# A two-layer trunk of matrix products: first stages in another order, and every large tile at a multiple of 512 bytes

## The chip, the cores and the metric

The kernel runs on one core of a Trainium2 chip. The metric is the device time of one execution in microseconds, lower is better. Before the change it is 2411.27 us, the median of three runs from 2409.95 to 2413.39.

## What is computed

Two layers work on 512 tokens of width 1024, all in float32. Each layer normalises x, projects it once into everything that follows, runs two token mixers on that (retention with four heads, and sparse attention with sixteen heads of width 64 in two groups), merges both by gates, adds the result to x and ends with a gated feed-forward part of width 2816. Cut to what matters:

```
h = rms_norm(x, norm_mix_g[i]);  proj = h @ w_in[i]
q_r, k_r, v_r, g_r, q_n, kv_n, gate_n, m_a, m_b = split(proj)
y_ret = (silu(g_r) * group_norm(retention(rotary(q_r), rotary(k_r), v_r))) @ w_o_ret[i]
y_nsa = nsa(q_n, kv_n (6 parts: compressed, selected, window keys and values), sigmoid(gate_n), ...) @ w_o_nsa[i]
x = x + (sigmoid(m_a) * y_ret + sigmoid(m_b) * y_nsa) @ w_out[i]
a, b = split(rms_norm(x, norm_ffn_g[i]) @ w_ffn_in[i])
x = x + (silu(a) * b) @ w_ffn_out[i]          # after two layers: rms_norm(x, norm_final_g)

def compress(kv, pos_emb, w1, w2):            # 31 overlapping blocks of 32 tokens
    flat = (blocks(kv) + pos_emb).reshape(..., 31, 32 * 64)
    return gelu(flat @ w1) @ w2
```

## The kernel before

Activations lie transposed: a tile holds 128 of the 1024 features (one of eight, called k) in its partitions and the 512 tokens along the free axis. Every product of float32 data is three matmuls (`mm3`, L122 to L124): each operand is split into a rounded part and the rest (hi and lo), and hi·hi, hi·lo and lo·hi are added up in one bank of PSUM. A product of 1024 features with 128 columns of weights is so 24 matmuls of 128x512. The split is `split` (L79 a copy on ScalarE, L80 a subtraction on VectorE), or `split_scaled` (L83, L84), which multiplies by the gain of the norm as well. The norm's other factor, one number per token, is applied behind the products by a multiplication with `rb`, a tile that holds it for all partitions. `norm_stats` makes the factor out of the summed squares (matmuls against ones, L216, and a power on GpSimd, L220), `norm_bcast` spreads it (a copy to `rep` on VectorE, L225, and four transposes on TensorE, L229).

Weights are loaded through SyncE's DMA queue (SP) into three buffers `wr` of up to 1 MB (`raw`, L91) and split into `wh` and `wl`, three buffers each (`cut`). Working tiles of 2 KB per partition share 37 slots (tag "u"); other tags (`p`, `pt`, `strip`, `mt`, `ld`, `cv`, `ks`) have their own. Within a partition the slots of "u", `p`, `pt` and `ks` begin 416 bytes past a multiple of 512, the weight buffers 96 past one, and `strip`, `mt`, `ld` and `cv` 160 past one: small tiles that are placed ahead of them set this.

The order of the work on each engine is settled when the program is built, by a scheduler that gives each engine its instructions in a row by their dependences and its own estimates; `issue_after` adds a dependence of order. The program's own order is the following. `start_x` (L232) loads x and the first weights (the 256 columns whose keys and values are compressed) and splits them. `nsa_kv` (L261) then makes the two products `psc` (banks "f"), calls `self.stats[0]` (bias rows at L176, squares by `acc_sq`, `norm_stats`), makes the key products `psk` (banks "a") with `norm_bcast` between them, and takes turns between the two compressions (`compress`, L323, for "k" and "v", whose matmuls are L362) and 18 steps of the first quad's q projection (`nsa_q`, L410, through `fill`). Each compression first builds z (L337) and xa (L348) on VectorE and splits xa into the tiles that its matmuls read. After that the sixteen heads run, four of them (a quad) on one q projection each; `nsa_q` gives for each half of a quad a hi and a lo tile of which one half of the partitions comes from a split, and the other half is copied from the first by L431. The first to read them are L441 and L442 in `nsa_cmp`. The bias of each head is a strip of 256 KB loaded on SP (L188). Retention, mixing and the feed-forward part follow; `proj_n` (L717) has the weights moving and the activations as stationary tile, all others the reverse.

Of the kernel before, what the change touches and what calls it, by code (L numbers as in the profile page):

```python
# [8 lines left out]
F32 = mybir.dt.float32  # L9
F32R = mybir.dt.float32r  # L10
AF = mybir.ActivationFunctionType
ALU = mybir.AluOpType
AX = mybir.AxisListType

P = 128
T = 512
D = 1024
NT = T // P
KD = D // P
# [3 lines left out]
HN = 16  # L23
# [8 lines left out]
class Builder:  # L32
# [86 lines left out]
    def mm3(self, ps, items, start=True, stop=True):  # L119
        n = len(items)  # L120
        for i, (lh, ll, rh, rl) in enumerate(items):
            self.nc.tensor.matmul(ps, lh, rh, start=start and i == 0, stop=False)  # L122
            self.nc.tensor.matmul(ps, lh, rl, start=False, stop=False)  # L123
            self.nc.tensor.matmul(ps, ll, rh, start=False, stop=stop and i == n - 1)  # L124

    def proj_t(self, w, j, acts, bank=None):

# [5 lines left out]
    def setup(self):  # L133
        nc, a = self.nc, self.a
        self.bv = self.dr.tile([HN, 640], F32, tag="bv", name="bv")
        self.cols = self.const("cols", [P, 104])
        nc.sync.dma_start(self.cols, a["c_cols"])
        self.gmix = [self.cols[:, l * 8 : l * 8 + 8] for l in range(DEPTH)]
        self.gffn = [self.cols[:, 16 + l * 8 : 24 + l * 8] for l in range(DEPTH)]
        self.pos = {"k": [self.cols[:, 40 + l * 16 : 56 + l * 16] for l in range(DEPTH)],  # L140
                    "v": [self.cols[:, 72 + l * 16 : 88 + l * 16] for l in range(DEPTH)]}
        self.ident = self.const("ident", [P, P])
        nc.gpsimd.dma_start(self.ident, a["c_ident"])
        self.setup_bias()
        self.mhalf = self.const("mhalf", [P, NT])
        nc.vector.memset(self.mhalf, -0.5)
        self.ones = self.const("ones", [P, 1])
        nc.vector.memset(self.ones, 1.0)
        self.rb = self.const("rb", [P, T])
        self.rstd = self.const("rstd", [P, NT])  # L150
        self.hrstd = self.const("hrstd", [P, NT])
        self.kcz = [self.const(f"kcz{g}", [P, 224], F32R) for g in range(2)]
        for g in range(2):
            nc.vector.memset(self.kcz[g].bitcast(F32), 0.0)
        self.xs = self.dr.tile([KD, P, T], F32, tag="xs", name="xs")
        self.gs = self.dr.tile([2 * KD, P, T], F32, tag="gs", name="gs")
        self.gr = self.dr.tile([4 * NSPILL, P, T], F32, tag="gr", name="gr")
        self.ys = self.dr.tile([KD, P, T], F32, tag="ys", name="ys")
        self.cmask = self.const("cmask", [P, NT, 32])
        nc.gpsimd.dma_start(self.cmask, a["c_cmask"].rearrange("p (i n) -> p i n", n=32))  # L160
# [71 lines left out]
    def start_x(self):  # L232

        nc = self.nc
        xts = [self.u("xt") for _ in range(KD)]
        w = self.a["w_in"][0][:, C_KV : C_KV + 256].rearrange("(k p) n -> p k n", p=P)
        for k in range(2):
            last = nc.sync.dma_start(xts[k], self.a["c_xt"][k])
        with self.tc.issue_after(last.ins):
            raw = self.raw([(lambda v: v, w)], KD, 256)  # L240
        with self.tc.issue_after(self.last_load.ins):
            for k in range(2, KD):
                self.last_x = nc.sync.dma_start(xts[k], self.a["c_xt"][k])
        h = [self.make_h(xts[k], self.gmix[0][:, k : k + 1]) for k in range(2)]
        with self.tc.issue_after(self.last_hi.ins):
            self.first_w = [self.cut(raw[:, :, j * P : (j + 1) * P]) for j in range(2)]
        h += [self.make_h(xts[k], self.gmix[0][:, k : k + 1]) for k in range(2, KD)]
        self.first_h = self.last_hi

        def stats():  # L250
            self.bias_rows()
            acc = None
            for xt in xts:
                acc = self.acc_sq(acc, xt)
            self.norm_stats(acc)

        self.stats = stats, self.norm_bcast
        return h


    def nsa_kv(self, l, h, q0):  # L261
        nc, w = self.nc, self.a["w_in"][l]
        view = lambda c, n, k0=0, kt=KD: w[k0 * P : (k0 + kt) * P, c : c + n].rearrange("(k p) n -> p k n", p=P)
        wc = self.first_w if l == 0 else self.wcols(w, 0, KD, C_KV, 256)
        psc = [self.proj_t(wc, j, h, "f") for j in range(2)]
        with self.tc.issue_after(self.last_x.ins) if l == 0 else nullcontext():
            wk = self.raw([(lambda v: v[:, :, :P], view(C_KV + 256, P)), (lambda v: v[:, :, P:], view(C_KV + 512, P))], KD, 256)
        self.stats[0]()
        nc.vector.tensor_scalar(self.hrstd, self.rstd, 0.5, None, ALU.mult)
        ks = [self.sb.tile([P, 2, T], F32R, tag=f"ks{g}", name=self.nm("ks"), bufs=1) for g in range(2)]  # L270

        def keys(br):
            kd, kh = self.u("kd"), self.u("kh", F32R)
            nc.vector.tensor_tensor(kd, psk[br], self.rb, ALU.mult)
            lo, hi = slice(0, 64), slice(64, P)
            self.split(ks[0][lo, br], ks[0][hi, br], kd[lo])
            self.split(kh[hi], ks[1][hi, br], kd[hi])
            nc.scalar.activation(ks[1][lo, br], kd[hi], AF.Copy)

        def values(half):  # L280
            return self.chunk([(lambda v: v[:, :, 0:P], view(C_KV + 384, P, half * 4, 4)),
                               (lambda v: v[:, :, P : 256 + 48], view(C_KV + 640, P + 48, half * 4, 4))], 4, 304, "k")

        with self.tc.issue_after(self.first_h.ins) if l == 0 else nullcontext():
            wk = [self.cut(wk[:, :, br * P : (br + 1) * P]) for br in range(2)]
        psk = [self.proj_t(wk, 0, h, "a")]
        self.stats[1]()
        psk.append(self.proj_t(wk, 1, h, "a"))
        comp = {kind: self.compress(l, kind, psc[i]) for i, kind in enumerate("kv")}
        fill = lambda n: [next(q0, None) for _ in range(n)]  # L290
        next(comp["k"])
        fill(9)
        next(comp["k"])
        next(comp["k"])
        next(comp["v"])
        keys(0)
        fill(9)
        next(comp["v"])
        next(comp["v"])
        keys(1)  # L300
        vs = [self.sb.tile([P, 4, 2, 64], F32R, tag="u", name=self.nm("vs")) for _ in range(NT)]
        gate = self.sb.tile([P, NT, HN, 3], F32, tag="gate", name=self.nm("gate"), bufs=1)
        pss = [self.bank(b) for b in "aaoo"]
        for half in range(2):
            wv = values(half)
            for t in range(NT):
                ts = slice(t * P, (t + 1) * P)
                self.mm3(pss[t][:, :304], [(h[half * 4 + k][0][:, ts], h[half * 4 + k][1][:, ts], wv[k][0], wv[k][1])
                                           for k in range(4)], start=half == 0, stop=half == 1)
            if half == 0:  # L310
                for kind in "kv":
                    next(comp[kind], None)
        for t in range(NT):
            src = pss[t][:, :256].rearrange("p (b d) -> p b d", d=64)
            rc = self.rstd[:, t : t + 1]
            nc.scalar.activation(vs[t][:, :, 0, :], src, AF.Copy, scale=rc)
            nc.vector.scalar_tensor_tensor(vs[t][:, :, 1, :], src, rc, vs[t][:, :, 0, :].bitcast(F32), ALU.mult, ALU.subtract)
            gt = gate[:, t].rearrange("p h b -> p (h b)")
            nc.scalar.activation(gt, pss[t][:, 256:304], AF.Tanh, scale=self.hrstd[:, t : t + 1])
            nc.vector.tensor_scalar(gt, gt, 0.5, 0.5, ALU.mult, ALU.add)  # L320
        return ks, vs, gate
# [88 lines left out]
    def nsa_q(self, l, h, quad, qs):  # L410
# [7 lines left out]
        for a in range(2):  # L418
# [7 lines left out]
            for g in range(2):  # L426
# [1 line left out]
                r, o = (slice(x * 64, x * 64 + 64) for x in (g, 1 - g))  # L428
                self.split(hi[r], lo[r], d[r])
                for x in (hi, lo):  # L430
                    nc.scalar.activation(x[o], x[r].bitcast(F32), AF.Copy)  # L431
                qs.append((hi, lo))
            yield

# [468 lines left out]
    def last_ffn(self, l, x, h):  # L903
# [3 lines left out]
        for hf in range(2):  # L907
            gf.append(self.tile("p", NPB))
            nc.sync.dma_start(gf[hf], self.a["norm_final_g"][None, hf * 512 : hf * 512 + 512].broadcast_to([P, 512]))
        ss = self.small("ss", 2 * NT)  # L910
        base = self.small("base", NT)
        for k0, kt in GROUPS:
            hid = self.hidden(l, h, k0, kt)
# [59 lines left out]
WR = 3  # L973
WH = 3
# [4 lines left out]
AT = {"scores": (0, 0.5), "values": (0, 0.8), "finish": (0.6, 0.6), "fill": (0.1, 0.7)}  # L979
QAT = (2, 2)  # L980
NSPILL = 3
FILL = [20, 18, 8, 8, 14, 14, 8, 8, 14, 14, 8, 8, 14, 14, 14, 14, 14, 12]
BANKS = {"a": 2, "o": 2, "t": 2, "f": 2}
CYCLE = "afo"
# [65 lines left out]
```

## Time and profile before

| | |
|---|---|
| median of three runs | 2411.27 us |
| the profiled execution | 2411.87 us |
| its span (first to last instruction) | 2409.8 us |
| TensorE busy | 2364.8 us, 98% |
| weight loads of TensorE | 1936.3 us, 80% |
| VectorE busy | 1386.1 us, 58% |
| ScalarE busy | 1070.7 us, 44% |
| GpSimd busy | 258.2 us, 11% |
| mean rate of the DMA engines | 108 GB/s |

Matmuls are pipelined, and their ends are modelled: one of 128x512 is shown with some 0.39 us, while the next starts earlier than that. The time that a stream of them needs is read from the distance between two starts, and not from the durations.

### The profile page before, as it was taken

The numbers are of one execution on the slowest core, as the hardware profiler recorded it, in microseconds if no ns is written. First come the engines' busy times: TensorE is split into PE (matmuls) and PEld (weight loads), VectorE is DVE, ScalarE is ACT, GpSimd is POOL, SyncE is SP. The second block draws the span as 40 slices with busy tenths as digits, with TensorE's granted clock in tenths as the row PEclk, the third lists the DMA queues.
The fourth block names the chain that finished last, engine by engine and source line by source line (L and its number), as shares of the span: only waits on it lengthen the run. The fifth ranks groups of instructions, "written<-read, shape, count | busy, mean of one in ns | idle before, by whom it ended". The sixth has DMA issues, their size and how long they took to land.

```text
span 2409.8 us, 29134 instructions
## 1 busy us (share of the span) xinstructions
PE 2364.8 (98%) x11042; PEld 1936.3 (80%) x11042; DVE 1386.1 (58%) x2715; ACT 1070.7 (44%) x1926; POOL 258.2 (11%) x224
## 2 busy tenths in 40 slices
PE   7999999999999999999989999999999999999998
PEld 5887778888887888888878777788888878888887
DVE  6777887354574633333577877864555754434344
ACT  5677786233333422222356777742433343322222
POOL 3000000010030110110200000001100202101010
PEclk9999999999999999999999999999999999999999
DMA  7532223522342522323444232244232533223221
GB/s 210 143 89 74 74 83 93 183 75 95 106 159 86 163 88 91 101 90 98 142 142 129 81 84 70 78 130 147 92 92 92 179 107 130 89 87 105 88 96 61
DMA packets 234172, 260.35 MB, mean 108 GB/s; under 512 B 42214, under 2 KB 178438, under 8 KB 234033
## 3 DMA queue, kind: packets, MB, share of 16 engines
q1 hardware_dynamic: 220688, 236.93, 32.3%
q10 hardware_dynamic: 13152, 21.37, 2.4%
q8 instruction: 86, 1.41, 0.2%
q14 instruction: 54, 0.43, 0.1%
q0 software_dynamic: 192, 0.21, 0.0%
HBM read 235.36 MB, written 23.11 MB: 107 GB/s over the span
## 4 chain that ended last, share of the span: by engine, by line
PE 90%; ACT 4%; DVE 4%; issue 1%; POOL 1%; DMA 0%; SPq 0%; ACTq 0%; POOLq 0%
PE f L122 12%; PE f L123 12%; PE f L124 12%; PE a L123 8%; PE a L122 8%; PE o L122 8%; PE o L123 8%; PE o L124 8%; PE a L124 8%; PE t L564 2%; PE o L556 1%; PE o L557 1%; ACT wh L79 1%; PE a L529 1%; PE a L530 1%
## 5 line engine op out<-in xcount | busy, mean ns | idle before, releaser
L79 ACT ACTIVATE wh<-wr 128x1024 fp32r<-128x1024 f32 (+3 forms) x406 | 397.9, 980 | 952.9 <-PE f L123 227.5
L80 DVE TENSOR_TENSOR wl<-wr,wh 128x1024 fp32r<-128x1024 f32 (+3 forms) x406 | 465.7, 1151 | 227.2 <-ACT wh L79 224.9
L122 PE MATMUL f<-hh,wh 128*128 128x512 f32 x936 | 373.1, 399 | 3.2 <-ACT wh L79 3.2
L123 PE MATMUL f<-hl,wh 128*128 128x512 f32 x936 | 369.9, 395 | 0.0
L124 PE MATMUL f<-hh,wl 128*128 128x512 f32 x936 | 368.1, 394 | 1.2 <-DVE wl L80 1.1
L124 PEld LDWEIGHTS f<-hh,wl 128*128 128x128 f32 x936 | 176.4, 188 | 41.9 <-DVE wl L80 3.6
L122 PEld LDWEIGHTS f<-hh,wh 128*128 128x128 f32 x936 | 176.4, 188 | 37.7 <-ACT wh L79 5.0
L123 PEld LDWEIGHTS f<-hl,wh 128*128 128x128 f32 x936 | 176.6, 189 | 30.7
L511 ACT ACTIVATE p<-p,nmx 128x512 f32<-128x512 f32 (+3 forms) x256 | 142.5, 557 | 53.7 <-DVE nmx L510 51.2
L80 DVE TENSOR_TENSOR pt<-t,pt 128x512 fp32r<-128x512 f32 (+3 forms) x256 | 123.2, 484 | 50.6 <-ACT pt L79 49.3
L874 POOL TENSOR_TENSOR fa<-fa,rb 128x512 f32<-128x512 f32 x44 | 77.6, 1763 | 562.2 <-ACT fa L873 562.2
L510 DVE CUSTOM_DVE_ANT_0 p<-a,strip 128x512 f32<-128x512 f32 (+3 forms) x256 | 119.4, 483 | 25.2 <-PE a L530 15.6
L123 PE MATMUL a<-hl,wh 128*128 128x512 f32 x336 | 132.4, 394 | 0.0
L122 PE MATMUL a<-hh,wh 128*128 128x512 f32 x336 | 132.4, 394 | 0.0
L124 PE MATMUL a<-hh,wl 128*128 128x512 f32 x336 | 131.2, 390 | 0.0
L79 ACT ACTIVATE pt<-t 128x512 fp32r<-128x512 f32 (+3 forms) x256 | 109.1, 427 | 47.6 <-PE t L564 43.5
L123 PE MATMUL o<-hl,wh 128*128 128x512 f32 x328 | 129.2, 394 | 0.0
L122 PE MATMUL o<-hh,wh 128*128 128x512 f32 x328 | 129.0, 393 | 0.0
L124 PE MATMUL o<-hh,wl 128*128 128x512 f32 x328 | 127.9, 390 | 0.0
L564 PE MATMUL t<-ident,p 128*128 128x128 f32 x640 | 113.9, 273 | 0.0
L564 PEld LDWEIGHTS t<-ident,p 128*128 128x128 f32 x640 | 81.2, 140 | 23.6 <-DVE pt L80 1.7
L556 PE MATMUL o<-pt,vs 128*128 128x512 f32 (+3 forms) x256 | 92.8, 365 | 3.2 <-ACT pt L79 3.2
(405 smaller groups left out, 4842.7 us busy)
## 6 DMA issues: line engine op xcount, KB each, us to landing
wr<-in_w_in SPq DMA_DIRECT2D x66, 1024.0 KB, 5.3
wr<-in_w_ffn_in SPq DMA_DIRECT2D x44, 1024.0 KB, 5.1
wr<-in_w_ffn_out SPq DMA_DIRECT2D x18, 1024.0 KB, 5.0
wr<-in_w_o_ret SPq DMA_DIRECT2D x16, 1024.0 KB, 5.0
wr<-in_w_in SPq DMA_DIRECT2D x36, 256.0 KB, 4.6
strip<-bv SPq DMA_DIRECT2D x32, 256.0 KB, 4.0
gs<-mt ACTq DMA_DIRECT2D x32, 256.0 KB, 2.0
wr<-in_w_o_nsa SPq DMA_DIRECT2D x16, 512.0 KB, 6.5
```

The lines of the kernel that those rows point to most:

```text
L79: self.nc.scalar.activation(hi, src, AF.Copy)
L80: (eng or self.nc.vector).tensor_sub(lo, src, hi.bitcast(F32))
L122: self.nc.tensor.matmul(ps, lh, rh, start=start and i == 0, stop=False)
L123: self.nc.tensor.matmul(ps, lh, rl, start=False, stop=False)
L124: self.nc.tensor.matmul(ps, ll, rh, start=False, stop=stop and i == n - 1)
L510: nc.vector.tensor_tensor_reduce(p, src, self.backwards(strip, w - 1, w), -1.0, BIG, ALU.add, ALU.min, nmx[:, c])
L511: nc.scalar.activation(p, p, AF.Exp, scale=-1.0, bias=nmx[:, c], accum_out=sm[:, c])
L529: nc.tensor.matmul(ps[:, :w], qh[:, ts], ks[:, br, :w], start=True, stop=False)
L530: nc.tensor.matmul(ps[:, :w], ql[:, ts], ks[:, br, :w], start=False, stop=True)
L556: nc.tensor.matmul(po[:, j * P :], lhs, th, start=br == 0 and j == 0, stop=False)
L564: nc.tensor.transpose(pt[:, (i - j) * P : (i - j + 1) * P], pr[br][i][:, j * P : (j + 1) * P], self.ident)
L874: nc.gpsimd.tensor_mul(t, t, self.rb)
```

## The change

The program is changed in six places.

1. Three pads (a constant of 96 bytes, a small tile of 48 floats, and `gate` widened to 256 floats), with one buffer number fixed (`ss`), move all large tiles to a multiple of 512 bytes within a partition.
2. At the start stand 32 matmuls of 224 columns on the zeroed tile `kcz`, whose result nobody reads; and a small copy on ScalarE (`hrstd`) comes before its other work.
3. `start_x` loads the first weights in four pieces of 256 KB between the x tiles, splits them in pairs of k, and `nsa_kv` goes through k with both banks instead of through one bank after the other (in layer 0).
4. In layer 0 the squares are added on VectorE instead of GpSimd; the norm's matmuls and the bias rows follow the first key product, the transposes the first half of the second. In layer 1 both stand between the two products `psc`.
5. In the compression stage v's blocks are built before k's third step, and the keys are written out later.
6. The 64 copies of q halves become DMAs on SP (L464 after the change).

```diff
 def setup(self):
+        self.const("pad", [P, 24])
+        self.small("pad", PAD, bufs=1)
         self.hrstd = self.const("hrstd", [P, NT])
+        nc.scalar.activation(self.hrstd, self.mhalf, AF.Copy)
+        ps = self.tp()
+        for _ in range(IDLE):
+            nc.tensor.matmul(ps[:, :224], self.kcz[0][:, :P], self.kcz[1], start=True, stop=True)
...
 def start_x(self):
-        for k in range(2):
-            last = nc.sync.dma_start(xts[k], self.a["c_xt"][k])
-        with self.tc.issue_after(last.ins):
-            raw = self.raw([(lambda v: v, w)], KD, 256)
+        for k in range(KD):
+            with order():
+                if k % 2 == 0:
+                    nc.sync.dma_start(raw[:, k : k + 2], w[:, k : k + 2])
+                xts.append(self.u("xt"))
                 self.last_x = nc.sync.dma_start(xts[k], self.a["c_xt"][k])
+            order = lambda: self.tc.issue_after(self.last_x.ins)
...
         def stats():
-            self.bias_rows()
             for xt in xts:
-                acc = self.acc_sq(acc, xt)
+                sq = self.u("sq")
+                nc.scalar.activation(sq, xt, AF.Square)
+                if acc is not None:
+                    nc.vector.tensor_add(sq, acc, sq)
+                acc = sq
             self.norm_stats(acc)
+            self.bias_rows()
...
 def nsa_kv(self, l, h, q0):
-        psc = [self.proj_t(wc, j, h, "f") for j in range(2)]
+        if l == 0:
+            psc = [self.bank("f") for _ in range(2)]
+            for k in range(KD):
+                for j in range(2):
+                    wh, wl = (v[:, j * P : (j + 1) * P] for v in self.first_w[k])
+                    self.mm3(psc[j], [(wh, wl, *h[k])], start=k == 0, stop=k == KD - 1)
+        else:
+            wc = self.wcols(w, 0, KD, C_KV, 256)
+            psc = [self.proj_t(wc, 0, h, "f")]
+            self.stats[0]()
+            psc.append(self.proj_t(wc, 1, h, "f"))
+            self.stats[1]()
-        self.stats[0]()
         psk = [self.proj_t(wk, 0, h, "a")]
-        self.stats[1]()
-        psk.append(self.proj_t(wk, 1, h, "a"))
+        if l == 0:
+            with self.tc.issue_after(self.last_mm.ins):
+                self.stats[0]()
+        psk.append(self.bank("a"))
+        for half in range(2):
+            part = range(4 * half, 4 * half + 4)
+            self.mm3(psk[1], [(wk[1][0][:, k], wk[1][1][:, k], *h[k]) for k in part], start=half == 0, stop=half == 1)
+            if l == 0 and half == 0:
+                with self.tc.issue_after(self.last_mm.ins):
+                    self.stats[1]()
         next(comp["k"])
         fill(9)
         next(comp["k"])
+        next(comp["v"])
         next(comp["k"])
-        next(comp["v"])
-        keys(0)
         fill(9)
         next(comp["v"])
         next(comp["v"])
+        keys(0)
         keys(1)
-        gate = self.sb.tile([P, NT, HN, 3], F32, tag="gate", name=self.nm("gate"), bufs=1)
+        gate = self.tile("gate", 1, w=256)[:, : NT * HN * 3].rearrange("p (t h b) -> p t h b", t=NT, h=HN)
...
 def nsa_q(self, l, h, quad, qs):
                 for x in (hi, lo):
-                    nc.scalar.activation(x[o], x[r].bitcast(F32), AF.Copy)
+                    nc.sync.dma_start(x[o].bitcast(F32), x[r].bitcast(F32))
...
+PAD = 48
+IDLE = 32
```

Three places show how instructions move. The first is SP's queue at its beginning (`cols` holds the gains; the numbers behind names count tiles), before:

```order
L137 DMA cols<-c_cols 128x104
L238 DMA xt_99<-c_xt 128x512
L238 DMA xt_100<-c_xt 128x512
L91 DMA wr_109<-in_w_in 128x8x256
L243 DMA xt_101<-c_xt 128x512
```

and after the change:

```order
L138 DMA cols<-c_cols 128x104
L248 DMA wr_135<-in_w_in 128x2x256
L250 DMA xt_137<-c_xt 128x512
L250 DMA xt_139<-c_xt 128x512
L248 DMA wr_135<-in_w_in 128x2x256
L250 DMA xt_142<-c_xt 128x512
```

The one load of 1 MB has become four of 256 KB, each ahead of two x tiles.

The second is VectorE in layer 0's compression stage, where the blocks of "v" are built (z and xa) and q's weights are split (wl); before, the last weight splits stand among z's operations and ahead of xa:

```order
L80 TENSOR_TENSOR ql_397<-qd_388,qh_396 64x512
L80 TENSOR_TENSOR wl_508<-wr_354,wh_507 128x1024
L369 TENSOR_TENSOR gx_455<-o_402,gy_456 64x256
L80 TENSOR_TENSOR wl_554<-wr_551,wh_553 128x1024
L371 TENSOR_SCALAR gy_456<-gy_456 64x256
L337 TENSOR_TENSOR z_466<-f_182,rb 64x256
L372 TENSOR_TENSOR gy_456<-gy_456,gx_455 64x256
L337 TENSOR_TENSOR z_466<-f_182,rb 64x256 x2
L374 SCALAR_TENSOR_TENSOR gy_456<-gy_456,gx_455 64x256
L337 TENSOR_TENSOR z_466<-f_182,rb 64x256
L348 TENSOR_TENSOR xa_471<-z_466,cols 128x4x31 x2
```

and after the change:

```order
L80 TENSOR_TENSOR ql_440<-qd_431,qh_439 64x512
L370 TENSOR_TENSOR z_474<-f_201,rb 64x256 x4
L381 TENSOR_TENSOR xa_479<-z_474,cols 128x4x31 x2
L381 TENSOR_TENSOR xa_486<-z_474,cols 128x4x31 x2
L381 TENSOR_TENSOR xa_493<-z_474,cols 128x4x31
L80 TENSOR_TENSOR pt_483<-xa_479,pt_483 128x4x64
L80 TENSOR_TENSOR pt_490<-xa_486,pt_490 128x4x64
L381 TENSOR_TENSOR xa_493<-z_474,cols 128x4x31
L381 TENSOR_TENSOR xa_500<-z_474,cols 128x4x31 x2
L402 TENSOR_TENSOR gx_533<-o_445,gy_534 64x256
L80 TENSOR_TENSOR pt_497<-xa_493,pt_497 128x4x64
L80 TENSOR_TENSOR pt_504<-xa_500,pt_504 128x4x64
```

wl_543, the split of the weights for q's second half, follows two rows further down (before, wl_508 has that place).

The third is SP's queue in the same stage, where the q copies (qh, ql) come in; before:

```order
L188 DMA strip_1424<-bv 128x512
L91 DMA wr_551<-in_cmp_w_v 128x8x256
L91 DMA wr_577<-in_cmp_w_v 128x8x256
L91 DMA wr_629<-in_w_in 128x4x128
L91 DMA wr_629<-in_w_in 128x4x176
```

and after the change:

```order
L91 DMA wr_586<-in_cmp_w_v 128x8x256
L195 DMA strip_1465<-bv 128x512
L195 DMA strip_1467<-bv 128x512
L464 DMA qh_433<-qh_433 64x512
L464 DMA ql_434<-ql_434 64x512
L464 DMA qh_439<-qh_439 64x512
L91 DMA wr_612<-in_cmp_w_v 128x8x256
L464 DMA ql_440<-ql_440 64x512
L91 DMA wr_672<-in_w_in 128x4x128
```

Four copies of the first quad's first half now stand ahead of or between the next weight loads.

## Rows read from the trace of the kernel before

**Rows 1.** The page: span, and each engine's busy time, share and instructions

```profile
span 2409.8 us, 29134 instructions
PE 2364.8 (98%) x11042; PEld 1936.3 (80%) x11042; DVE 1386.1 (58%) x2715; ACT 1070.7 (44%) x1926; POOL 258.2 (11%) x224
```

**Rows 2.** The chain that ended last: start us, us, what

```profile
2.12 8.59 DMA wr<-in_w_in
...
57.38 2.35 DVE xa L348 x8
60.46 1.33 DVE pt L80 x4
```

**Rows 3.** Timeline, first 16 us: start us, us, instruction, [idle before, releaser]

```profile
1.01 0.48 DVE L154 MEMSET kcz<- 128x224 f32 x2
...
8.29 1.00 PE L176 MATMUL t<-ohv,tab 33*16 33x256 f32 x2 [8.29 <-DMA ohv<-c_ohv]
...
11.84 0.80 PE L122 MATMUL f<-hh,wh 128*128 128x512 f32 x1 [2.55 <-ACT wh L79]
...
15.39 0.59 PE L123 MATMUL f<-hl,wh 128*128 128x512 f32 x1
...
15.82 0.40 PE L124 MATMUL f<-hh,wl 128*128 128x512 f32 x1
```

**Rows 4.** Windows: stretch, its length, engines' busy time, granted clock, DMA share, GB/s

```profile
core 0: us, PE busy (x) PEld busy (x) DVE busy (x) ACT busy (x) POOL busy (x), PEclk, DMA share, GB/s
0.00:12.00 12.00, 1.17 (x3) 0.30 (x3) 2.22 (x8) 3.89 (x5) 3.13 (x9) 1.00 0.84 281
57.40:70.40 13.00, 7.90 (x36) 7.45 (x36) 12.61 (x23) 10.65 (x17) 0.00 (x0) 0.61 0.20 53
```

**Rows 5.** Timeline, 25 to 40 us, TensorE

```profile
25.16 0.40 PE L122 MATMUL a<-hh,wh 128*128 128x512 f32 x1
...
36.61 0.66 PE L229 MATMUL t<-ident,rep 128*128 128x128 f32 x4 [1.80 <-DVE rep L225]
...
39.83 0.47 PE L122 MATMUL f<-hh,wh 128*128 128x512 f32 x1
```

**Rows 6.** Waits: engine, line, waited for, us in total, times, longest

```profile
PE o L362 <- DVE pt L80: 6.2, 2, 3.1
PE o L362 <- DVE wl L80: 6.1, 6, 2.5
...
PE o L556 <- ACT pt L79: 3.2, 8, 0.5
...
PE f L442 <- ACT ql L431: 0.2, 1, 0.2
...
SPq L91 <- DVE wl L80: 1430.6, 165, 21.1
```

**Rows 7.** Line 431: count, ns min/median/max, first and last start

```profile
L431 ACT ACTIVATE ql<-ql x32: 608/630/634, 48.5 to 1512.4; 64x512 fp32r<-64x512 f32 x32
```

**Rows 8.** DMA issues: count, KB each, median us from issue to landing

```profile
strip<-bv SPq DMA_DIRECT2D x32, 256.0 KB, 4.0
```

**Rows 9.** Timeline of TensorE at full clock: first and last of equally spaced matmuls

```profile
480.24 0.39 PE L122 MATMUL o<-wh,hh 128*128 128x512 f32 x1
...
482.33 0.39 PE L122 MATMUL o<-wh,hh 128*128 128x512 f32 x1
...
511.56 0.39 PE L122 MATMUL f<-p,pt 128*128 128x512 f32 x1
...
512.92 0.39 PE L122 MATMUL f<-p,pt 128*128 128x512 f32 x1
...
905.17 0.39 PE L122 MATMUL f<-hh,wh 128*128 128x512 f32 x1
...
907.23 0.39 PE L122 MATMUL f<-hh,wh 128*128 128x512 f32 x1
...
2214.65 0.40 PE L122 MATMUL a<-hh,wh 128*128 128x512 f32 x1
...
2216.05 0.40 PE L122 MATMUL a<-hh,wh 128*128 128x512 f32 x1
```

More of the change, by code (lines that the diff above doesn't have):

```diff
@@ L123, in mm3 @@
             self.nc.tensor.matmul(ps, lh, rl, start=False, stop=False)
-            self.nc.tensor.matmul(ps, ll, rh, start=False, stop=stop and i == n - 1)
+            self.last_mm = self.nc.tensor.matmul(ps, ll, rh, start=False, stop=stop and i == n - 1)
     def proj_t(self, w, j, acts, bank=None):
@@ L234, in start_x @@
         nc = self.nc
-        xts = [self.u("xt") for _ in range(KD)]
         w = self.a["w_in"][0][:, C_KV : C_KV + 256].rearrange("(k p) n -> p k n", p=P)
-        for k in range(2):
-            last = nc.sync.dma_start(xts[k], self.a["c_xt"][k])
-        with self.tc.issue_after(last.ins):
-            raw = self.raw([(lambda v: v, w)], KD, 256)
-        with self.tc.issue_after(self.last_load.ins):
-            for k in range(2, KD):
-                self.last_x = nc.sync.dma_start(xts[k], self.a["c_xt"][k])
@@ L244, in start_x @@
[L244 to L247, printed above, removed]
+        raw = self.wp.tile([P, 2048], F32, tag="wr", name=self.nm("wr"), bufs=WR).rearrange("p (k n) -> p k n", k=KD)
+        xts, h, self.first_w, order = [], [], [], nullcontext
+        for k in range(KD):
[3 more added lines that the diff above has]
+                xts.append(self.u("xt"))
+                self.last_x = nc.sync.dma_start(xts[k], self.a["c_xt"][k])
+            order = lambda: self.tc.issue_after(self.last_x.ins)
@@ new lines, in start_x @@
+        for k in range(0, KD, 2):
+            if k % 4 == 0:
+                hi, lo = (self.wp.tile([P, 1024], F32R, tag=t, name=self.nm(t), bufs=WH).rearrange("p (k n) -> p k n", k=4)
+                          for t in ("wh", "wl"))
+            with self.tc.issue_after(self.last_hi.ins) if k else nullcontext():
+                self.split(hi[:, k % 4 : k % 4 + 2], lo[:, k % 4 : k % 4 + 2], raw[:, k : k + 2])
+            self.first_w += [(hi[:, k % 4 + i], lo[:, k % 4 + i]) for i in range(2)]
+            h += [self.make_h(xts[k + i], self.gmix[0][:, k + i : k + i + 1]) for i in range(2)]
@@ L263, in nsa_kv @@
         view = lambda c, n, k0=0, kt=KD: w[k0 * P : (k0 + kt) * P, c : c + n].rearrange("(k p) n -> p k n", p=P)
-        wc = self.first_w if l == 0 else self.wcols(w, 0, KD, C_KV, 256)
-        psc = [self.proj_t(wc, j, h, "f") for j in range(2)]
+        if l == 0:
[10 more added lines that the diff above has]
+            self.stats[1]()
         with self.tc.issue_after(self.last_x.ins) if l == 0 else nullcontext():
             wk = self.raw([(lambda v: v[:, :, :P], view(C_KV + 256, P)), (lambda v: v[:, :, P:], view(C_KV + 512, P))], KD, 256)
-        self.stats[0]()
-        nc.vector.tensor_scalar(self.hrstd, self.rstd, 0.5, None, ALU.mult)
         ks = [self.sb.tile([P, 2, T], F32R, tag=f"ks{g}", name=self.nm("ks"), bufs=1) for g in range(2)]
@@ L286, in nsa_kv @@
         psk = [self.proj_t(wk, 0, h, "a")]
-        self.stats[1]()
-        psk.append(self.proj_t(wk, 1, h, "a"))
+        if l == 0:
[8 more added lines that the diff above has]
+                    self.stats[1]()
+        nc.vector.tensor_scalar(self.hrstd, self.rstd, 0.5, None, ALU.mult)
         comp = {kind: self.compress(l, kind, psc[i]) for i, kind in enumerate("kv")}
@@ L909, in last_ffn @@
             nc.sync.dma_start(gf[hf], self.a["norm_final_g"][None, hf * 512 : hf * 512 + 512].broadcast_to([P, 512]))
-        ss = self.small("ss", 2 * NT)
+        ss = self.small("ss", 2 * NT, bufs=2)
         base = self.small("base", NT)
```

## The prediction

> **What bounds the kernel now.** I read the page first: TensorE is busy 2364.8 of 2409.8 us, 98%, while VectorE has 58% and ScalarE 44% [rows 1]. What can be won is therefore of two kinds: the 45 us in which TensorE does nothing, or the time of one matmul step. Next I read the chain of waits from its start, to see which of the idle time ends last: the chain begins with 8.59 us of waiting for the first weight load [rows 2]. Then came the timeline of the first 40 us, for what TensorE does there. The first real matmul starts at 11.84; two neighbours at 15.39 and 15.82 stand 0.43 us apart, about twice the full-speed step, and the later one is the first that is modelled at 0.40 us instead of 0.59 (the clock's column says 1.00 for the first 12 us [rows 4]; I go by the steps); the key projection starts at 25.16 and the first q projection at 39.83 [rows 3, 5]. The windows show where the clock falls: from 57.4 to 70.4 TensorE is busy 7.90 of 13 us and the granted clock is 0.61 of full, so part of that stretch ran at 1.2 GHz and not at 2.4 [rows 4]. The waits of TensorE name the same place, the first compression matmuls (L362), 6.2 and 6.1 us over both layers [rows 6]. Last I compared starts of neighbouring matmuls at full clock in four stages, for the step: it is not the same everywhere [rows 9].
>
> **The start.** Before, one 1 MB load must land and be split whole before TensorE can begin at 11.84. Now the load comes in four pieces between the x tiles, and 48 matmuls (8 k, 2 columns, 3 products) follow k by k. Ahead of them stand 32 matmuls of 224 columns on the zeroed tile, which is ready at about 1.5 (1.01 + 0.48) [rows 3]. At the slow step these cost 224/512 × 0.43 = 0.188 us each, 6.0 in all, to 7.5; if the clock rises after 4 us of them, as it did between the first matmul at 11.84 and 15.82, the last eleven cost half of that and the end is 6.6. The first x tile and its piece of weights are 256 KB each; issued by 1.5, landing some 4.0 us later as another 256 KB do [rows 8], and split in 0.6 each (a copy of 64x512 takes 0.63 [rows 7]), they are ready at 6.7 or so, when the idle matmuls end. I take 7.0 for the first real matmul. At 0.233 each, 48 take 11.2 us, so the stage ends at 18.2 where it ended at 25.16: **−7.0**. Are the data there? x and weights are 3.1 MB, 11 us at the 281 GB/s of the first 12 us [rows 4], so the last pair lands near 13 and is split near 14; TensorE wants it after 36 matmuls, at 15.4. If it came at 16.5, 1.1 us would go. So −5 to −8.
>
> **The key projection and the norm.** From 25.16 to 39.83 is 14.67 us for 48 matmuls (11.2), the rest being the norm's matmuls, its transposes and a wait of 1.80 for the replicated scale [rows 5]. The squares now add on VectorE, the norm matmuls go right behind the first projection and the transposes behind half of the second, so six matmul steps of cover stand in front of the transposes and the 1.80 should go. On the other side the bias matmul, which ran at 8.29 in an idle engine (1.00) [rows 3], now stands on the path, and the eight squares and adds lie on VectorE beside the splits of the second weights: I put 0.3 on that. −1.80 + 1.0 + 0.3 = **−0.5**, between −1.8 (nothing of the additions shows) and +1.3 (the wait stays, too). In layer 1 the same steps move between two projections that have cover on both sides: 0.
>
> **The compression stage, both layers.** Here 6.2 + 6.1 us of waits stand [rows 6], and the slow clock behind them [rows 4]. The change builds v's blocks before the second fill of q matmuls. But VectorE's rows now read z (4), xa (8) and pt (4), with gx and gy, before the split of the weights for q's second half (wl_543). The eight xa operations are 2.35 us before and the four splits of pt 1.33 [rows 2]; with the z and g operations it comes to about 7 us. Those weights are what TensorE needs next, so the wait moves from v's blocks to q's weights. I take **0** for both layers. The bound below is that all of it goes, −12.3; above, that TensorE waits the whole 7 us where it waited 6, in both layers, and stays at the slow clock 2 us longer, +5. The nearest row is the one of the same VectorE work (2.35), which is not shorter after the change, and that is why I take neither end.
>
> **The q copies.** 64 copies of 64x512 leave ScalarE: 64 × 0.63 = 40 us of an engine that is at 44% [rows 1, 7]. TensorE waited for ScalarE's pt only 3.2 us in all [rows 6], so at best −3.2. Each copy becomes a 128 KB DMA in SP's queue, among the weight loads. A 256 KB strip takes 4.0 us from issue to landing [rows 8]; a DMA that waits for its split holds the next weight load back, but weights are loaded two buffers ahead (SP's queue itself waits 1430.6 us for buffers, 8.7 each time [rows 6]), so that is covered. The first matmuls on a quad's q (L441, L442) come soon after the copies. The later six quads could lose 4.0 − 2 × 0.63 = 2.7 each, 16 in all; but other matmuls stand between in the new order. From −3.2 to +16, I take **0**, nearest to the 0.2 us that TensorE waited for these copies [rows 6]. The Trainium skill (SBUF — State Buffer, Door 1: The DMA port swizzle) says that 64 partitions reach half of the ports, so that such a transfer gets half of the rate; no row here has a transfer onto 64 partitions, and it speaks for the upper end.
>
> **Placement.** All large tiles lay at 416, 96 or 160 bytes past a multiple of 512; now all lie at 0. Can it change the step? With the weights moving (96, against 416) nine steps take 2.09 us, 232 ns; the retention output, where both tiles lie at 416, has six in 1.36, 227; the FFN, activations at 416 against weights at 96, has nine in 2.06, 229; but the same kind of product at 2214 has six in 1.40, 233 [rows 9]. The last pair speaks against a rule by these offsets alone, since offsets were equal and the step was not. I take **0** for it and make both ends rivals. The Trainium skill (TensorE: Matmul & The Clock Gate, Back-to-back issue gap) gives N/2.4 + 2.5 for one matmul alone, 216 ns here; each row is 11 to 17 ns above it. If placement were all of that, an estimate by the page is some 8,300 × 13 ns, 110 us less; no row shows a step so short.
>
> **The sum.** −7.0 − 0.5 + 0 + 0 + 0 = −7.5. The profiled execution took 2411.87 us (span 2409.8 and 2.1 around it), 0.6 above the median of the runs, 2411.27. 2411.87 − 7.5 = 2404.4, and by the median's place 2403.8: I say **2404**. The likeliest case's own range is 2397 (compression gives half of its waits back) to 2411 (the q copies and the norm cost some).
>
> **Rivals.** (1) Placement lowers the step: where moving and stationary tiles lie at the same offset it is 227 ns now, and after the change they all do. By the source, some 6,860 steps stream activations and 1,488 stream weights; 6,860 × 2.2 ns (229 to 226.7) + 1,488 × 6.6 ns (233.3 to 226.7) = 25 us, so 2379. For it speaks the order of the three stages; against it 2214. Chance 0.25. (2) The opposite: a moving and a stationary tile at one offset get in each other's way and every step becomes the longest one seen, 233: 6,860 × 4.4 ns = +30, so 2434, slower. For it: 233 exists for the common kind, and which of the two a stretch has is not explained; against it: equal offsets of 416 had the shortest step. Chance 0.09. It decides from 1.8 ns per step on, where it eats the whole gain and the bound beside it. (3) The q DMAs come late: a copy lands behind a weight load in SP's queue, and the quad's first matmuls wait 2.7 us each time: 2404 + 16 = 2420, slower. The place is the first two matmuls on a new quad's q, and it decides from 2 us per quad on. For it: TensorE waited for a copy at L442 even when it took 0.63 [rows 6, 7]; against: 0.2 us in all is what that came to. Chance 0.1. (4) That the idle matmuls do not raise the clock: the start then keeps about 2 us of half-speed steps, and the time is 2406; it lies in the likeliest case. That case has 0.56.
>
> **How the numbers follow.** A change under 0.2% (4.8 us) cannot be told from none here, so faster means below 2406.4 and slower above 2416.1. Faster: all of rival 1 (0.25) and 0.72 of the likeliest case (0.40), 0.65. Slower: rivals 2 and 3 (0.19) and a little of the likeliest, 0.2. The rest, 0.15, is within. For 8 in 10 the range must hold the likeliest case, rival 1 and half of rival 3: 2375 to 2419, leaving out the deep end of rival 1, half of rival 3 and rival 2.
>
> **What would show it.** Right at the start: first real matmul near 7, the key projection's first at 18 (against 25.16), no 0.42 us steps among real matmuls. Norm: no wait for the replicated scale above 0.5 us. Compression: waits at L362's successor of about 6 us over both layers for pt or wl, and a granted clock below 1.00 in a window after 50 us. q copies: ScalarE's busy time lower by about 40 us, no L464 among the releasers of more than 1 us. Placement: the steps of the four stages as they were, within 1 ns. Wrong I am if any stage's step has moved by 2 ns or more, which over 8,300 steps outweighs everything else here.

## The result and the profile after

The changed kernel takes 2384.22 us, the median of four runs (2383.37 to 2384.80), against 2411.82 for the kernel before in the same session; the ratio is 0.9883, 95% interval 0.9871 to 0.9895. That is 27.6 us less, inside the range of the prediction and 20 us below its number, 2404. The time of the placement rival, 2379, is nearer than that of the case I called likeliest.

The page after, the span and the line of busy times, to be read beside [rows 1]:

```profile
span 2381.6 us, 29325 instructions
PE 2345.2 (98%) x11074; PEld 1941.9 (82%) x11074; DVE 1380.3 (58%) x2724; ACT 1034.8 (43%) x1865; POOL 249.3 (10%) x217
```

TensorE's share is the same 98%, and it has 32 matmuls more, yet its busy time is 20 us shorter. ScalarE has 36 us less, the q copies. The first question is therefore the step, which the same four stages show as in [rows 9]; first and last start of equally spaced matmuls, after the change:

```profile
471.72 0.39 PE L122 MATMUL o<-wh,hh 128*128 128x512 f32 x1
...
473.76 0.39 PE L122 MATMUL o<-wh,hh 128*128 128x512 f32 x1
...
501.76 0.39 PE L122 MATMUL f<-p,pt 128*128 128x512 f32 x1
...
503.12 0.39 PE L122 MATMUL f<-p,pt 128*128 128x512 f32 x1
...
890.17 0.39 PE L122 MATMUL f<-hh,wh 128*128 128x512 f32 x1
...
892.21 0.39 PE L122 MATMUL f<-hh,wh 128*128 128x512 f32 x1
...
2200.34 0.39 PE L122 MATMUL o<-hh,wh 128*128 128x512 f32 x1
...
2201.70 0.39 PE L122 MATMUL o<-hh,wh 128*128 128x512 f32 x1
```

Nine steps in 2.04, six in 1.36, nine in 2.04, six in 1.36: 226.7 ns in each stage. The four different steps of before (232, 227, 229, 233) have become one, and it is the shortest of the four.

The timeline of the start, to be read beside [rows 3, 5]:

```profile
1.53 5.69 PE L161 MATMUL t<-kcz,kcz 128*128 128x224 f32 x32 [1.53 <-DVE kcz L157]
...
7.06 0.40 PE L122 MATMUL f<-hh,wh 128*128 128x512 f32 x1
...
17.98 0.39 PE L122 MATMUL a<-hh,wh 128*128 128x512 f32 x1
...
30.89 0.42 PE L122 MATMUL f<-hh,wh 128*128 128x512 f32 x1
```

The first real matmul is at 7.06 (forecast 7.0), already at 0.40 and not 0.59 to 0.80; the key projection begins at 17.98 (forecast 18.2) and q's first matmul at 30.89, where it was 39.83.

The waits of TensorE, us in total, times and longest, beside [rows 6]:

```profile
PE f L124 <- DVE wl L80: 6.5, 2, 3.3
PE o L395 <- DVE pt L80: 5.7, 2, 2.9
PE o L590 <- DVE pt L80: 2.8, 2, 1.4
PE f L474 <- DMA qh<-qh: 2.1, 2, 1.0
PE f L475 <- DMA ql<-ql: 1.8, 2, 1.1
PE t L236 <- DVE rep L232: 1.5, 2, 0.8
...
PE o L395 <- DVE wl L80: 1.4, 4, 0.5
```

In the compression stage 13.4 us of waits (6.2 and 6.1 at L362 [rows 6], and 1.1 at L124) have become 13.6 (5.7, 6.5 and 1.4): v's blocks are still awaited, and q's weights (L124) in place of most of the second kind. The copies of q now appear as a releaser, which they hardly did before (0.2). Where these waits stand in layer 0, by the timeline (VectorE's split of q's weights among them):

```profile
44.99 0.39 PE L395 MATMUL o<-wh,pt 128*128 128x256 f32 x1 [2.90 <-DVE pt L80]
...
47.36 1.21 DVE L80 TENSOR_TENSOR wl<-wr,wh 128x1024 fp32r<-128x1024 f32 x1
...
48.63 0.80 PE L124 MATMUL f<-hh,wl 128*128 128x512 f32 x1 [3.25 <-DVE wl L80]
49.22 0.63 PE L122 MATMUL f<-hh,wh 128*128 128x512 f32 x1
49.65 0.63 PE L123 MATMUL f<-hl,wh 128*128 128x512 f32 x1
```

TensorE waits 2.90 us, then 3.25, and what follows runs at 0.43 us a step. The clock fell here as it did before [rows 4]. The window of that stretch (columns as there, TensorE alone; 0.80 is the mean of its part at 2.4 GHz and its part at 1.2):

```profile
40.00:57.00 17.00, 10.34 (x43) 0.80 0.66 186
```

The two timelines set side by side by the first matmul of each stage (us, before and after, and what each stage gained):

| stage | before | after | stage's own gain, layer 0 and layer 1 |
|---|---|---|---|
| first compression matmul | 45.42 | 36.41 | start, projections, norm −9.0 |
| first score matmul | 85.77 | 76.69 | compression −0.1; layer 1 with its projections +0.3 |
| output projection of attention | 414.31 | 406.44 | heads **+1.2**; +1.5 |
| layer 1's first projection | 1206.61 | 1189.37 | retention, mixing, feed-forward −9.4; −13.0 |
| last matmul | 2402.85 | 2374.39 | total −28.5 |

The stages whose code is unchanged but for one buffer number (retention, mixing, feed-forward) gave 22.4 of 28.5 us. The attention heads became slower.

### The profile page after: what moved, and what is told of

Its sections match the earlier page's. It is cut to its first block, busy times and chain, and to the rows that moved or that the text cites. A ratio compares the mean times of both kernels' runs of the same rounds, so it can differ in the third digit from the quotient of the medians.

```text
span 2381.6 us, 29325 instructions
## 1 busy us (share of the span) xinstructions
PE 2345.2 (98%) x11074; PEld 1941.9 (82%) x11074; DVE 1380.3 (58%) x2724; ACT 1034.8 (43%) x1865; POOL 249.3 (10%) x217
## 4 chain that ended last, share of the span: by engine, by line
PE 94%; DVE 2%; ACT 1%; DMA 1%; POOL 1%; issue 1%; SPq 0%; POOLq 0%; ACTq 0%
PE f L122 12%; PE f L124 12%; PE f L123 12%; PE a L123 7%; PE a L122 7%; PE o L122 7%; PE o L124 7%; PE a L124 7%; PE o L123 7%; PE t L597 3%; PE o L590 2%; PE o L589 2%; PE a L562 1%; PE a L563 1%; DMA ql<-ql 1%
## 5 line engine op out<-in xcount | busy, mean ns | idle before, releaser
L79 ACT ACTIVATE wh<-wr 128x1024 fp32r<-128x1024 f32 (+2 forms) x408 | 398.5, 978 | 934.6 <-PE f L123 237.2
L80 DVE TENSOR_TENSOR wl<-wr,wh 128x1024 fp32r<-128x1024 f32 (+2 forms) x408 | 462.8, 1137 | 206.0 <-ACT wh L79 202.9
L124 PE MATMUL f<-hh,wl 128*128 128x512 f32 x936 | 369.2, 395 | 6.5 <-DVE wl L80 6.5
L124 PEld LDWEIGHTS f<-hh,wl 128*128 128x128 f32 x936 | 177.1, 189 | 44.5 <-DVE wl L80 6.9
L543 DVE CUSTOM_DVE_ANT_0 p<-a,strip 128x512 f32<-128x512 f32 (+3 forms) x256 | 119.7, 484 | 35.9 <-PE a L563 27.6
L124 PE MATMUL a<-hh,wl 128*128 128x512 f32 x336 | 130.8, 389 | 0.0
L124 PE MATMUL o<-hh,wl 128*128 128x512 f32 x328 | 127.6, 389 | 0.0
```

Source lines behind the costliest of these rows:

```text
L79: self.nc.scalar.activation(hi, src, AF.Copy)
L80: (eng or self.nc.vector).tensor_sub(lo, src, hi.bitcast(F32))
L124: self.last_mm = self.nc.tensor.matmul(ps, ll, rh, start=False, stop=stop and i == n - 1)
L543: nc.vector.tensor_tensor_reduce(p, src, self.backwards(strip, w - 1, w), -1.0, BIG, ALU.add, ALU.min, nmx[:, c])
```

## The experiments

Each run stands beside runs of the kernel before on the same chip (medians 2410.3 to 2411.1).

**The pads, taken out of the changed kernel (no_pads), and put alone into the kernel before (pads_only).**

```diff
-        self.const("pad", [P, 24])
-        self.small("pad", PAD, bufs=1)
...
-        gate = self.tile("gate", 1, w=256)[:, : NT * HN * 3].rearrange("p (t h b) -> p t h b", t=NT, h=HN)
+        gate = self.sb.tile([P, NT, HN, 3], F32, tag="gate", name=self.nm("gate"), bufs=1)
...
-        ss = self.small("ss", 2 * NT, bufs=2)
+        ss = self.small("ss", 2 * NT)
```

> The changed kernel with its three pads taken out: the redone first stages, the idle matmuls and the q copies as DMAs stay, the large tiles go back to 416, 96 and 160 bytes past a multiple of 512. If placement alone shortened the steps behind the first stages (about -5 us in each retention stage, -3.5 and -7.3 in the two feed-forward stages, some 22 in all between the two traces), this runs at 2384 + 22 = 2406 us, its steps are 229 and 233 ns again, and its first stages keep their 9 us. If the order or the copies did it (other phases of the engines against each other), it stays near 2385 with steps of 227 ns.

> The kernel before with the three pads alone: all large tiles at a multiple of 512, nothing moved. Placement theory: every step of 128x512 in retention, mixing and feed-forward is 227 ns and the time falls by 22 us, to 2390; the first real matmul stays at 11.8. Rival, placement only works together with the new order: 2408 or more, and steps of 229 and 233 ns.

no_pads takes 2406.87 us (ratio to before 0.9985, 0.9976 to 0.9994), pads_only 2388.10 (0.9905, 0.9891 to 0.9918). The same product in both, attention's output projection, first and last start, no_pads and then pads_only:

```profile
435.97 0.39 PE L122 MATMUL f<-oh,wh 128*128 128x512 f32 x1
...
438.03 0.39 PE L122 MATMUL f<-oh,wh 128*128 128x512 f32 x1
```

```profile
436.25 0.39 PE L122 MATMUL a<-oh,wh 128*128 128x512 f32 x1
...
437.61 0.39 PE L122 MATMUL a<-oh,wh 128*128 128x512 f32 x1
```

Nine steps in 2.06 (229 ns) without the pads, six in 1.36 (227) with them. Placement is worth 22.7 us on the changed kernel (2406.87 − 2384.22) and 22.2 on the kernel before (2410.31 − 2388.10): it gives the same with the rest of the change and without it. All else in the change is worth only 3.4 us (2410.31 − 2406.87) or 3.9 (2388.10 − 2384.22) together. The changed kernel was timed in another session than the other three, and the kernel before had 2411.82 there and 2410.31 here; a difference across sessions is good to some 1.5 us.

**Which placement counts: all tiles at 32 (all_32), the weights alone at 32, 128 and 256 (w_32, w_128, w_256).** The edits are one number each: the first pad shifts all large tiles, the second the weight tiles alone.

```diff
-        self.const("pad", [P, 24])
+        self.const("pad", [P, 32])      # all_32
...
-PAD = 48
+PAD = 56                                # w_32; 80 in w_128, 112 in w_256
```

> The changed kernel with its first pad 32 bytes larger: all large tiles now lie 32 bytes past a multiple of 512, moving and stationary tiles still at the same offset. If it is the equal offset that counts, the steps stay at 227 ns and the time at 2384. If the tiles must begin at a multiple of 64 bytes or more, the steps are 229 to 233 ns and the time 2400 to 2410.

> The changed kernel with the second pad 32 bytes larger: working tiles stay at 0, the weight tiles wh and wl lie at 32 past a multiple of 512. If the moving and the stationary tile have to lie at the same offset, steps with weights are 229 to 233 ns and the time some 2400 to 2406, while the retention output (both tiles at 0) keeps 227. If only the working tiles' place counts, 2385.

> As the run with the weights at 32, but with the weight tiles at 256 past a multiple of 512. If equal offsets are needed only modulo 256 (or 64), steps of 227 ns and 2385; if modulo 512, 229 to 233 ns and 2400 to 2406.

> The changed kernel with the weight tiles at 128 past a multiple of 512 and the working tiles at 0. A distance of 256 gave 227 ns, one of 32 gave 233, and before the change the distance was 192 modulo 256. If the distance has to be a multiple of 128, steps of 227 ns and 2385; if of 256, 229 to 233 ns and 2400 to 2430.

all_32 takes 2385.58 us (2384.69 to 2386.54), w_256 2384.24 (2384.00 to 2384.49), w_32 2429.90 (2429.31 to 2430.49), w_128 2425.97 (2424.61 to 2427.33). Nine steps of the output projection in each, in the order all_32, w_256, w_32, w_128:

```profile
436.00 0.39 PE L122 MATMUL a<-oh,wh 128*128 128x512 f32 x1
...
438.04 0.39 PE L122 MATMUL f<-oh,wh 128*128 128x512 f32 x1
```

```profile
435.86 0.39 PE L123 MATMUL f<-ol,wh 128*128 128x512 f32 x1
...
437.90 0.39 PE L123 MATMUL f<-ol,wh 128*128 128x512 f32 x1
```

```profile
436.06 0.40 PE L122 MATMUL f<-oh,wh 128*128 128x512 f32 x1
...
438.16 0.40 PE L122 MATMUL f<-oh,wh 128*128 128x512 f32 x1
```

```profile
435.82 0.39 PE L122 MATMUL a<-oh,wh 128*128 128x512 f32 x1
...
437.91 0.40 PE L122 MATMUL a<-oh,wh 128*128 128x512 f32 x1
```

2.04, 2.04, 2.10 and 2.09 us: 227, 227, 233 and 232 ns. In w_32 the retention output, which reads two working tiles, must keep its step if it is the distance that counts; six steps of it in that run:

```profile
506.12 0.39 PE L123 MATMUL f<-p,pt 128*128 128x512 f32 x1
...
507.48 0.39 PE L123 MATMUL f<-p,pt 128*128 128x512 f32 x1
```

They take 1.36 us, 227 ns, in the same run in which the products with weights take 233. Where the tiles lie does not count by itself (all at 32 is as good as all at 0), and the multiple of 512 of the change's title is not needed. What counts is the distance between the moving and the stationary tile: 0 and 256 gave the short step, 32, 128 and (before the change) 192 modulo 256 the long ones. Of the distances tried, those are short that are a multiple of 256 bytes. What a bad distance costs was put too low in w_32's expectation (2400 to 2406), which is the price at the distance of before: in w_32 every product with weights has 233 ns, and it is 46 us slower than the changed kernel, and 19 slower than the kernel before, from a shift of 32 bytes.

**The q copies, back on ScalarE (q_on_scalar), and as DMAs in the kernel before (before_q_dma).**

```diff
-                    nc.sync.dma_start(x[o].bitcast(F32), x[r].bitcast(F32))
+                    nc.scalar.activation(x[o], x[r].bitcast(F32), AF.Copy)
```

> The changed kernel with the 64 q copies back on ScalarE instead of as DMAs on SP. Between the two traces the attention stage lost about 1.3 us in each layer (from the first score matmul to the output projection) although its steps can only have become shorter. If the q DMAs are late (TensorE waits 2.1 and 1.8 us for qh and ql), this runs 2.5 to 4 us faster than the changed kernel, 2380 to 2382. Rival, the copies on ScalarE cost as much through the waits for pt (3.2 us before): 2384 to 2387.

> The kernel before with only the 64 q copies made into DMAs on SP. If late DMAs cost by themselves, this is slower than before by 2 us or more, 2413 to 2418 (half of it in the attention stages). If they cost only together with the new compression order, it is 2410 to 2412, the same as before.

q_on_scalar takes 2377.59 us (2377.09 to 2377.83; ratio to before 0.9861, 0.9847 to 0.9874): 6.6 us less than the changed kernel, more than the 2.5 to 4 expected, and the fastest version of all. before_q_dma takes 2410.18 (0.9994, 0.9985 to 1.0003), the same as before: there the DMAs cost nothing on balance. Its TensorE waits 4.3 us for them where before it waited 0.2 for the copies, and the wait for v's pt is 1.6 where it was 6.2 [rows 6]:

```profile
PE f L442 <- DMA ql<-ql: 2.8, 2, 1.6
...
PE o L362 <- DVE pt L80: 1.6, 2, 1.1
PE f L441 <- DMA qh<-qh: 1.5, 2, 0.8
```

By its timeline the heads are 0.7 and 1.0 us longer than before in the two layers, and the compression stages 1.2 and 1.1 shorter. In the changed kernel the DMAs cost 6.6 us on balance, so something comes with them there that is not their landing alone. By the stages of the two timelines, 4.4 us of it lie in the two compression stages (2.56 and 1.86) and 3.0 in the heads (1.4 and 1.6), while the start is 0.9 shorter. The waits of q_on_scalar, beside those of the changed kernel above:

```profile
PE o L395 <- DVE wl L80: 8.4, 10, 1.4
...
PE f L124 <- DVE wl L80: 1.1, 2, 0.5
```

The wait for v's pt is gone from the list, that for q's weights (L124) is 1.1 and not 6.5, and that for the compression's weights (L395) is 8.4 and not 1.4: 9.5 us in place of 13.6. The row of VectorE in the compression stage shows what differs for q's weights (the line with + stands at this place only in q_on_scalar; cut behind xa):

```
 L80 TENSOR_TENSOR ql_440<-qd_431,qh_439 64x512
+L80 TENSOR_TENSOR wl_543<-wr_397,wh_542 128x1024
 L370 TENSOR_TENSOR z_474<-f_201,rb 64x256 x4
 L381 TENSOR_TENSOR xa_479<-z_474,cols 128x4x31 x2
```

With the copies on ScalarE the scheduler puts the split of q's second weights ahead of v's z and xa again; with the DMAs it puts it behind them, and TensorE waits for it.

**The compression stage's old order, with the DMAs (cmp_old) and with ScalarE copies (old_and_scalar).**

```diff
         next(comp["k"])
-        next(comp["v"])
         next(comp["k"])
+        next(comp["v"])
+        keys(0)
         fill(9)
         next(comp["v"])
         next(comp["v"])
-        keys(0)
         keys(1)
```

> The changed kernel with the compression stage's order of before (v's blocks built after k's third step, keys between); the q copies stay DMAs. In VectorE's row the split of the weights for q's second half then stands ahead of v's z and xa again. If the 3.25 us for which TensorE waits for that split in each layer come from the new order, this is faster than the changed kernel by up to 5 us, 2379 to 2382. If, as I forecast, one wait only takes the place of another (v's blocks late instead of q's weights), it is within 2 us of 2384.

> The changed kernel with both the compression stage's old order and the q copies on ScalarE; the start, the norm's new place and the pads stay. The two undone one at a time gave 2380.3 and 2377.6 against 2384.2. If they cost independently (4 for the order, 6.6 for the DMAs), both together give 2373.7. If the DMAs cost mainly by the row of VectorE that comes with them (in the run with ScalarE copies the split of q's weights stands ahead of z and xa again, without the old order), the two overlap and the time is 2376 to 2379.

| | copies as DMAs | copies on ScalarE |
|---|---|---|
| new compression order | 2384.22 (the change) | 2377.59 |
| old compression order | 2380.28 | 2380.61 |

My forecast for cmp_old, within 2 us of 2384, was wrong; the first theory there (2379 to 2382) holds. With the old order it makes no difference that the times can show where the copies are made; by these medians the new order gains 3.0 us with copies on ScalarE and loses 3.9 with DMAs. The four stand in different sessions; as ratios to the kernel before in each they are 0.9883 (the change), 0.9861 (q_on_scalar), 0.9873 (cmp_old) and 0.9878 (old_and_scalar), each to about 0.0013, and only the difference between the first two is clear of this. The two compression stages together (layer 1's with its projections), by the timelines, take 108.9 us in the changed kernel, 104.5 in q_on_scalar, 105.8 in cmp_old and 109.1 in old_and_scalar, which is the same crossing. The two do not add: independent costs would have given 2373.7, and even the band given for an overlap, 2376 to 2379, was too low. TensorE's compression waits in old_and_scalar are those of before, in their kind and nearly in their size [rows 6]:

```profile
PE o L395 <- DVE wl L80: 6.4, 6, 3.0
PE o L395 <- DVE pt L80: 4.7, 2, 3.1
```

In these four the new order is good, then, where the weights' split stays ahead of v's blocks, and bad where it does not. The changed kernel also loses 1.2 and 1.5 us in the heads, and cmp_old, which has the same DMAs, does not in layer 0 (85.77 to 414.31 before is 328.5, 75.72 to 404.25 in cmp_old 328.5) and hardly in layer 1 (0.3). The waits on qh and ql are not the difference: 3.9 us in the one, 3.6 in the other (1.4 and 2.2). The granted clock is. Windows of TensorE within the heads of both layers, the changed kernel and then cmp_old (all of its heads); the clock is the number behind the count in parentheses:

```profile
176.20:179.40 3.20, 3.20 (x13) 0.50 0.00 0
1357.20:1360.40 3.20, 3.20 (x12) 0.50 0.00 0
```

```profile
75.00:405.00 330.00, 324.56 (x1675) 1.00 0.34 97
1253.00:1584.00 331.00, 325.42 (x1679) 1.00 0.34 96
```

In the changed kernel TensorE works at 1.2 GHz for 3.2 us in the heads of each layer, where 2.4 GHz would have done the same in half of the time: some 1.6 us. It comes behind a wait of 1.4 us for pt (the 2.8 at L590 above). cmp_old has that wait too and keeps its clock, and in all_32 and no_idle the clock falls in layer 0 alone (heads of 330.5 and 330.0 us there, 329.4 and 329.0 in layer 1). Beside this the heads with DMAs are up to 1.0 us longer than before where the clock holds (before_q_dma). Why it falls in the one and not in the other stays open.

**The idle matmuls, left out (no_idle).**

```diff
-IDLE = 32
+IDLE = 0
```

> The changed kernel without the 32 idle matmuls at the start. If they raise the clock ahead of the real work, the real matmuls now begin slowly (0.43 us steps for some 4 us, as before the change) and the start loses 1.5 to 2.5 us: 2386 to 2387. If the first 48 matmuls wait for x and weights anyway, so that a slow start is made up, nothing: 2384.

no_idle takes 2385.78 us (2384.48 to 2385.88; ratio 0.9895, 0.9878 to 0.9911). Its start on the timeline:

```profile
6.49 0.80 PE L122 MATMUL f<-hh,wh 128*128 128x512 f32 x1 [6.49 <-ACT hh L83]
...
8.30 0.63 PE L122 MATMUL f<-hh,wh 128*128 128x512 f32 x1
8.73 0.63 PE L123 MATMUL f<-hl,wh 128*128 128x512 f32 x1
...
11.15 0.39 PE L123 MATMUL f<-hl,wh 128*128 128x512 f32 x1
11.38 0.39 PE L124 MATMUL f<-hh,wl 128*128 128x512 f32 x1
```

Without them the real matmuls begin earlier, at 6.49, take 0.43 us a step until about 11, and reach the first compression matmul at 38.18 instead of 36.41: 1.8 us, as forecast. The idle matmuls do raise the clock ahead of the work. In the whole time the difference (1.6) lies at the edge of what the intervals can tell. What the load in four pieces, the copy on ScalarE and the norm's new place give was not tested one by one.

## Why the prediction was right, and where it was not

- **The start: right.** 7.06 and 17.98 against 7.0 and 18.2, a gain of 7.2 where −7.0 stood. The data were there in time: no matmul among the 48 waited.
- **Key projection and norm: sign right, size short.** From 17.98 to 30.89 is 12.91 us, against 14.67: −1.8, the end of the term's range, where −0.5 stood. The wait for the replicated scale shrank to 0.8 and did not go (1.5 over both layers), but the bias matmul, which I had put on the path with 1.0 us, took 0.60 at full clock, and the 48 steps took 10.9 and not 11.2 us.
- **Compression: right in size, and for this row in mechanism.** The waits were exchanged, 13.4 for 13.6, and q's weights took the place named; the half-speed steps stayed. But I took this for a property of the new order. It is one of the row that the scheduler made of it together with the DMAs; in q_on_scalar the same order has another row, and its compression stages are 4.4 us shorter.
- **q copies: the size was missed.** The term was 0, between −3.2 and +16. On the changed kernel it is +6.6, and on the old compression order and on the kernel before 0 within the intervals. The prediction looked for their cost in the landing of a DMA (2.1 + 1.8 us of waits came, against 0.2) and not in VectorE's row, which comes out in another order with them (4.4 us), nor in the clock, which falls in the heads.
- **Placement: this step failed.** "I take **0** for it and make both ends rivals." The argument was that the same kind of product, at the same offsets, had 229 ns at 905 and 233 at 2214. The runs show that at a bad distance the step is not one number. Before the change the products with the weights moving have 233.3 ns on average, while most of those with the activations moving repeat steps of some 226, 229 and 232, mean 229; but the whole stretch from 2160 to 2256, in which the row at 2214 lies, stands at 233 to 234. In no_pads, at the same offsets, the same kind of product in that stretch has 229 again (nine steps in 2.06):

```profile
2208.08 0.39 PE L122 MATMUL a<-hh,wh 128*128 128x512 f32 x1
...
2210.14 0.39 PE L122 MATMUL a<-hh,wh 128*128 128x512 f32 x1
```

With a good distance no such stretch is left behind the heads: the means of these products lie between 226.6 and 227.4 in pads_only, all_32, w_256 and the changed kernel. (Within the heads, where products of several kinds alternate, stretches with a mean of 231 to 232 remain with the pads too.) The two rows of one kind with two steps were therefore a mark of bad placement, and I read them as evidence against it. Rival 1 had the right rule in its first clause (equal offsets) and nearly the right price: 25 us forecast, 22.7 and 22.2 measured. The attention heads gave nothing of it: from the first score matmul to the output projection layer 0 takes 328.5 us before and 328.4 in pads_only; the scores and outputs there read two working tiles, which lay at one offset already. The Trainium skill (TensorE: Matmul & The Clock Gate, Back-to-back issue gap) has 216 ns for one matmul alone. With the tiles at equal offsets this trace stays at 226.7, so placement did not remove the other 11.

By the runs' medians the change is made up so: the pads −22.2 (2410.31 to 2388.10), the start and the norm −7.5 (to 2380.61, old_and_scalar), the new compression order −3.0 (to 2377.59), the DMAs on top of it +6.6 (to 2384.22). The −7.5 of the forecast is that of the second step alone. (The timelines give the first stages 9.0 and not 7.5: the start of the kernel before moves by itself, with the first compression matmul at 45.42 in its trace and at 43.14 in that of pads_only, whose first stages have the same code.) Without the pads the changed kernel takes 2406.87, near the forecast's 2404. Placement, which I set to 0, is what moved the time, and the range held it because rival 1 was in it, not because the sum was right.

## What to carry to other kernels

Print the address of the moving and the stationary tile of a long stream of matmuls and keep their distance a multiple of 256 bytes (0 and 256 were tried): a pad of 32 bytes ahead of a pool cost 46 us here, or 2%, with no instruction changed. When equal products run at unequal steps, look at placement first, and do not judge it from a few steps in two places. And when a scheduler makes the rows, an engine that is relieved can change the order on another: test a relief together with the order that it lives in.

## What was not expected of the hardware

A float32 stream of 128x512 matmuls of one kind has a step of 226.7 ns, flat, when the two tiles' addresses differ by 0 or 256 bytes. It has 233 ns when the weights lie 32 bytes past the activations' offset and 232 to 233 at 128. At the distance of before (stationary less moving tile, modulo 256) it has 233 ns at 64, where the weights move, and 229 at 192, where they stand, but for one stretch of some 100 us at 233. Why that stretch differs is open, as is every distance that was not tried. A DMA of 64 partitions by 2 KB within the core's memory landed 2.9 (qh) and 3.1 us (ql) after its issue in the changed kernel, medians of 32 each, where a 256 KB strip from outside took 3.5; in no_pads it was 3.2 and 4.5, with 3.7 for the strip. Half of the bytes did not land much sooner, and in no_pads ql landed later.
